# Dividing the first load of a decoder step between two DMA queues

## The chip, the cores and the metric

The kernel runs on one core of a Trainium2 chip. The metric is the device time of one execution in microseconds (us); the time of a version is the median of its runs.

## The reference: what is computed

One layer of a hybrid decoder for 256 prompt tokens and 8 sample tokens, 264 columns in all, with D = 2048, in float32:

```python
xn = rms_norm(x, g_mix);  z = xn @ w_in          # 2048 -> 3584, split among three mixers
y_pool = pool_mixer(...) @ w_pool_br             # trailing windows 2, 4, 8, 16
y_lru  = (rg_lru(causal_dwconv(u_lru)) * gelu(u_gel)) @ w_lru_br
y_conf = silu(layer_norm(causal_dwconv(c_a * sigmoid(c_b)))) @ w_conf_br
g_a, g_b, g_c = split(sigmoid(xn @ w_gate + b_gate), 3)
x = x + (g_a * y_pool + g_b * y_lru + g_c * y_conf) @ w_out
x = x + square(relu(rms_norm(x, g_mlp) @ w_up)) @ w_down      # 2048 -> 8192 -> 2048
y = rms_norm(x, g_final)
```

The outputs are y for both kinds of tokens and the new states of the mixers.

## The kernel before

Activations lie with features on the 128 partitions and the 264 tokens (N) along the row; x is 16 tiles of 128 x 264 (KD = 16). All weights are one stream of 478 chunks in the order of use, mostly of 1024 columns (CH): a pair of 128 x 512 pieces each. Every float32 product is made of three matmuls of a reduced type: the weights are split into `whi` (ScalarE, a cast, L170) and `wlo` (VectorE, the rest, L171), the activations likewise into A's upper and lower half (`x_tile`, L302 to L305). So a chunk goes HBM -> `raw` (six buffers of 1024 columns) -> ScalarE's cast -> VectorE's subtraction -> TensorE. `split(j)` does it for chunk j, three chunks ahead of its use. The order is written out by hand, per engine in program order.

The first four chunks are of kind "dual": each is one 128-row slice of w_in for two groups of 512 columns, multiplied with one tile of x as soon as it is there (`dual_mm`, L927). It takes the columns 0 to 511 first, then 512 to 1023; for each half four matmuls of whi with A's upper half, four of whi with its lower half, four of wlo with the upper half. Ahead of them stand eight warm-up products on constants (L320, two records each).

The first loads come from a DRAM array of their own, in the order of the list `HEAD`. Its entries: ("h", a, b) is columns a to b of a head row that holds g_mix (16 columns), x's first tile (264) and columns 0 to 511 of chunk 0; it goes to the last buffer of `raw`. (c, a, b) is columns a to b of chunk c; ("x", a, b) is x's tiles a to b, which go to `GX`. Eight transfers are in flight at most: a later issue waits for the one eight before it. `dma_head` issues entries, all on SyncE's queue (L156): the first ten without a wait, the others while the first chunks are split. From chunk 10 on `dma_pair(p)` brings chunks 2p and 2p + 1 (L138), in one transfer of 1 MB where both have 1024 columns, else one by one (L145). Chunks of 512 columns are 34, 37, 40, 42 (the gate blocks of the RG-LRU) and 64, which stands beside an empty one.

GpSimd copies g_mix out of the head (`gmix`, L325); VectorE prepares the first tile of x (L302), ScalarE the upper half of the others (L304).

Of the kernel before, what the change touches and what calls it, by code (L numbers as in the profile page):

```python
# [15 lines left out]
P = 128  # L16
# [3 lines left out]
N = TP + TS  # L20
KD = D // P
# [23 lines left out]
CH = 1024  # L45
# [3 lines left out]
WARM = 8  # L49
DUAL = 4  # L50
AHEAD = 3
HEAD = [("h", 0, KD + N + 256), ("h", KD + N + 256, KD + N + 512), (0, 512, CH), ("x", 1, 2)]
for _c in (1, 2):
    HEAD += [(_c, 0, 512), (_c, 512, CH), ("x", _c + 1, _c + 2)]
for _c in range(3, 9):
    HEAD += [(_c, 0, CH), ("x", 2 * _c - 2, 2 * _c)]
HEAD += [(9, 0, CH), ("x", 0, 1)]


def weight_plan():  # L60

    groups = [("w_in", 0, 16, m) for m in (1, 2, 0, 3, 4, 6, 5)]
    for g in range(4):
        groups += [("w_gate", 0, 16, t) for t in ((0, 4, 1), (5,), (2, 6), (3, 7))[g]]
        groups += [("w_pool_br", 0, 4, g), ("w_lru_br", 0, 8, g)]
    for g in range(4):
        groups += [("w_gate", 0, 16, 8 + g)]
        groups += [("w_conf_br", 0, 4, m) for m in ((), (), (0, 1), (2, 3))[g]]  # L70
    groups += [("w_out", 0, 16, m) for m in range(4)]
    for q in range(4):
        groups += [("w_up", 0, 16, q * 4 + m) for m in range(4)]
        groups += [("w_down", q * 16, 16, m) for m in range(4)]
    chunks = [("dual", 0, k, CH) for k in range(DUAL)]
    for gi, (name, _, k, m) in enumerate(groups):
        for c in range(DUAL // 2 if gi < 2 else 0, k // 2):
            chunks.append(("dense", gi, c, CH))
            if name == "w_in" and (m, c) in LRU_AT:
                chunks.append(("lru", LRU_AT.index((m, c)), 0, 512))  # L80
            if (name, m) == ("w_gate", 0) and c == 3:
                chunks += [("grp", 0, 0, 512), ("none", 0, 0, 0)]
    return groups, chunks
# [3 lines left out]
def hybrid_step(ctx: ExitStack, tc: tile.TileContext, first_in, par_in, st_in, wall, y_out, st_out):  # L87
    nc = tc.nc
# [8 lines left out]
    raw = cpool.tile([P, NRAW, CH], F32, name="raw")  # L97
# [23 lines left out]
    def acc():  # L121
        return psum.tile([P, 512], F32, name="acc", tag="acc")
# [7 lines left out]
    groups, chunks = weight_plan()  # L130
    n_pairs = len(chunks) // 2

    def dma_pair(p):
        s = (2 * p) % NRAW
        if p >= n_pairs:
            return
        if chunks[2 * p][3] == chunks[2 * p + 1][3] == CH:
            nc.sync.dma_start(raw[:, s:s + 2, :], wall[p].rearrange("p (a c) -> p a c", a=2))  # L138
        else:
            for h in range(2):  # L140
                if chunks[2 * p + h][3]:
                    dma_part(2 * p + h, 0, chunks[2 * p + h][3])

    def dma_part(c, a, b):
        nc.sync.dma_start(raw[:, c % NRAW, a:b], wall[c // 2, :, c % 2 * CH + a:c % 2 * CH + b])  # L145

    at = [0]

    def dma_head(n):
        for kind, a, b in HEAD[n]:  # L150
            if kind == "x":
                to = GX[:, KD * (a > 0) + a * N:KD + b * N]
            else:
                to = raw[:, NRAW - 1 if kind == "h" else kind % NRAW, a:b]
            w = to.shape[1]
            nc.sync.dma_start(to, first_in[at[0]:at[0] + P * w].rearrange("(p w) -> p w", p=P))  # L156
            at[0] += P * w

    head = raw[:, NRAW - 1, :]
# [149 lines left out]
        nc.vector.tensor_tensor(lo, x, f(hi), op=ALU.subtract)  # L309


    nc.scalar.preload_act_table_set(LN_EXP)
    early = HEAD.index((5, 0, CH))
    dma_head(slice(0, early))
    nc.vector.memset(ones, 1.0 / D)
    nc.vector.memset(f(ones_r), 1.0 / D)
    nc.vector.memset(eps, EPS)
# [529 lines left out]
    def half(h):  # L847
        return slice(h * (N // 2), (h + 1) * (N // 2))
# [98 lines left out]
    for a in (0, 512):  # L947
        split(2, slice(a, a + 512))
    x_tile(3)
    dma_head(slice(early, -2))  # L950
    dual = [[acc() for _ in range(4)] for _ in range(2)]
    pss = None
    for i, ch in enumerate(chunks):
# [5 lines left out]
        if i == 0:  # L959
            dma_head(slice(-2, None))  # L960
        elif i % 2 == 0:
            dma_pair((i + 8) // 2)
# [6 lines left out]
        kind, gi, c, _ = ch  # L969
# [51 lines left out]
    early = acc()  # L1021
# [4 lines left out]
    c = half(1)  # L1026
    nc.scalar.activation(total[:, c], ps[1][:, c], AF.Identity, bias=eps)
    nc.scalar.activation(X[:, KD - 1, :], X[:, KD - 1, :], AF.Copy, scale=gfin[:, KD - 1:KD])
    c = half(0)
    nc.vector.scalar_tensor_tensor(t[:, c], ps[0][:, c], EPS, sq[:, c], op0=ALU.add, op1=ALU.mult)  # L1030
    nc.vector.scalar_tensor_tensor(early[:, c], t[:, c], -3.0, rstd[:, c], op0=ALU.add, op1=ALU.mult)  # L1031
    c = half(1)
# [108 lines left out]
```

## Time and profile before

| | |
|---|---|
| time, median of 3 runs | 1300.82 us (1300.23 to 1300.83) |
| profiled execution | 1300.82 us, its span 1299.0 us |
| TensorE busy | 1288.3 us (99%) |
| VectorE, ScalarE, GpSimd busy | 837.9, 717.7, 96.9 us |
| mean clock of TensorE by the records | 0.998 |
| moved by DMA | 257.10 MB, mean 198 GB/s |

The profile counts a matmul from its start to a modelled end, so a busy TensorE may still wait for its pipeline; the spacing of its instructions tells more. "PEld" is its weight load. "SPq" and "ACTq" rows are DMA issues on SyncE's and ScalarE's queue; the landing shows in the row of the engine that waited for it. Rows of a timeline give start and length in us from the span's start, engine, line, operation, output <- input, shape, count, and in brackets how long the engine stood idle before and what ended that.

### The profile page before, as it was taken

To read this page: it belongs to the slowest core of one execution; us is meant where nothing else is said; L and a number is where in the kernel's file an instruction comes from. 1 tells how busy PE (TensorE), PEld (TensorE's weight loads), DVE (VectorE), ACT (ScalarE), POOL (GpSimd) and SP (SyncE) were. 2 spreads that over 40 slices of the span, in tenths; PEclk is the share of its full clock that TensorE was granted. 3 is DMA by queue.
4 is the path that set the end of the run, shared out by engine and by line. 5 is a ranking of instruction groups with operands and counts; after the bars stand their busy time and mean duration, and the time that the engine had idled before them with its cause. 6 is when DMAs were issued, how large, how long until landed. Compare 5 with 4: busy or idle time off the path is not lost.

```text
span 1299.0 us, 26651 instructions
## 1 busy us (share of the span) xinstructions
PE 1288.3 (99%) x11420; PEld 1287.7 (99%) x11420; DVE 837.9 (64%) x1060; ACT 717.7 (55%) x1017; POOL 96.9 (7%) x118
## 2 busy tenths in 40 slices
PE   9999999999999999999999999999999999999996
PEld 9999999999999999999999999999999999999996
DVE  7886898776777687666655455655555655555554
ACT  7767677667674655455544334543344533354544
POOL 0430010110101032021000000000000000000012
PEclk9999999999999999999999999999999999999999
DMA  9646555555655555655555555555555555555551
GB/s 360 214 169 208 188 210 200 196 194 196 228 193 198 187 182 195 217 188 201 197 196 196 195 197 196 196 190 203 196 195 196 196 197 196 196 197 196 195 197 70
DMA packets 39431, 257.10 MB, mean 198 GB/s; under 512 B 4368, under 2 KB 5648, under 8 KB 10000
## 3 DMA queue, kind: packets, MB, share of 16 engines
q1 hardware_dynamic: 38592, 253.21, 55.4%
q8 instruction: 89, 1.46, 0.4%
q10 hardware_dynamic: 576, 1.15, 0.2%
q0 software_dynamic: 144, 1.04, 0.2%
q14 instruction: 30, 0.25, 0.0%
HBM read 252.18 MB, written 3.21 MB: 197 GB/s over the span
## 4 chain that ended last, share of the span: by engine, by line
PE 99%; DVE 0%; ACT 0%; DVEq 0%; issue 0%; ACTq 0%
PE acc L195 33%; PE acc L194 33%; PE acc L193 33%; PE acc L927 1%; DVE raw L1041 0%; PE acc L320 0%; DVEq L1120 0%; PE acc L293 0%; ACT rstd L1024 0%; ACT G L1025 0%; DVE acc L1031 0%; ACT G L859 0%; DVE G L1030 0%; DVE GX L854 0%; DVE G L857 0%
## 5 line engine op out<-in xcount | busy, mean ns | idle before, releaser
L171 DVE TENSOR_TENSOR wlo<-raw,whi 128x1024 fp32r<-128x1024 f32 (+1 forms) x482 | 587.7, 1222 | 441.5 <-ACT whi L170 435.8
L170 ACT CAST whi<-raw 128x1024 fp32r<-128x1024 f32 (+1 forms) x482 | 496.4, 1032 | 530.3 <-PE acc L194 482.4
L195 PE MATMUL acc<-A,wlo 128*128 128x264 f32 x1824 | 503.4, 276 | 0.0
L194 PE MATMUL acc<-A,whi 128*128 128x264 f32 x1824 | 503.4, 276 | 0.0
L193 PE MATMUL acc<-A,whi 128*128 128x264 f32 x1824 | 503.4, 276 | 0.0
L193 PEld LDWEIGHTS acc<-A,whi 128*128 128x128 f32 x1824 | 344.7, 189 | 0.0
L194 PEld LDWEIGHTS acc<-A,whi 128*128 128x128 f32 x1824 | 344.7, 189 | 0.0
L195 PEld LDWEIGHTS acc<-A,wlo 128*128 128x128 f32 x1824 | 344.7, 189 | 0.0
L194 PE MATMUL acc<-xn,whi 128*128 128x264 f32 x1024 | 282.6, 276 | 0.0
L195 PE MATMUL acc<-xn,wlo 128*128 128x264 f32 x1024 | 282.6, 276 | 0.0
L193 PE MATMUL acc<-xn,whi 128*128 128x264 f32 x1024 | 282.6, 276 | 0.0
L193 PE MATMUL acc<-LH,whi 128*128 128x264 f32 x768 | 212.0, 276 | 0.0
L195 PE MATMUL acc<-LH,wlo 128*128 128x264 f32 x768 | 212.0, 276 | 0.0
L193 PEld LDWEIGHTS acc<-xn,whi 128*128 128x128 f32 x1024 | 193.5, 189 | 0.0
L195 PEld LDWEIGHTS acc<-xn,wlo 128*128 128x128 f32 x1024 | 193.5, 189 | 0.0
L194 PEld LDWEIGHTS acc<-xn,whi 128*128 128x128 f32 x1024 | 193.5, 189 | 0.0
L194 PE MATMUL acc<-Q,whi 128*128 128x264 f32 x644 | 177.7, 276 | 0.0
L193 PEld LDWEIGHTS acc<-LH,whi 128*128 128x128 f32 x768 | 145.2, 189 | 0.0
L195 PEld LDWEIGHTS acc<-LH,wlo 128*128 128x128 f32 x768 | 145.2, 189 | 0.0
L194 PEld LDWEIGHTS acc<-Q,whi 128*128 128x128 f32 x644 | 121.7, 189 | 0.0
L822 POOL TENSOR_TENSOR G<-G 128x264 f32<-128x264 f32 x28 | 25.5, 911 | 746.5 <-ACT G L820 745.5
L194 PE MATMUL acc<-LH,whi 128*128 128x264 f32 x256 | 70.7, 276 | 0.0
(197 smaller groups left out, 832.2 us busy)
## 6 DMA issues: line engine op xcount, KB each, us to landing
raw<-wall_dram SPq DMA_DIRECT2D x229, 1024.0 KB, 4.8
raw<-first_dram SPq DMA_DIRECT2D x7, 512.0 KB, 8.2
raw<-wall_dram SPq DMA_DIRECT2D x4, 512.0 KB, 3.7
GX<-first_dram SPq DMA_DIRECT2D x6, 264.0 KB, 7.7
raw<-first_dram SPq DMA_DIRECT2D x5, 256.0 KB, 5.0
raw<-wall_dram SPq DMA_DIRECT2D x5, 256.0 KB, 2.8
so_dram<-st POOLq DMA_DIRECT2D x1, 1018.0 KB, 6.0
st<-st_dram SPq DMA_DIRECT2D x1, 912.0 KB, 9.4
```

The costliest lines, as they stand in the source:

```text
L170: nc.scalar.copy(h[:, s], r[:, s])
L171: nc.vector.tensor_tensor(lo[:, s], r[:, s], f(h[:, s]), op=ALU.subtract)
L193: nc.tensor.matmul(ps[:, :N], whi_t, xh, start=first, stop=False)
L194: nc.tensor.matmul(ps[:, :N], whi_t, xl, start=False, stop=False)
L195: nc.tensor.matmul(ps[:, :N], wlo_t, xh, start=False, stop=last)
L822: nc.gpsimd.tensor_tensor(sq2, sq2, t, op=ALU.add)
L927: nc.tensor.matmul(ps[:, :N], w[:, k % NHI, b * P:(b + 1) * P], sent(x), start=first, stop=False)
```

## The change

The head's first entry is cut in two: g_mix and x's first tile (280 columns), issued on ScalarE's queue ahead of its activation table load, and the first 256 columns of weights, issued first on SyncE's queue. Two further entries, x's second tile and columns 0 to 511 of chunk 1, are issued on ScalarE's queue too, behind the table load. `dma_pair` brings a pair whose first chunk is full and whose second has 512 columns in one transfer.

```diff
-HEAD = [("h", 0, KD + N + 256), ("h", KD + N + 256, KD + N + 512), (0, 512, CH), ("x", 1, 2)]
+HEAD = [("h", 0, KD + N), ("h", KD + N, KD + N + 256), ("h", KD + N + 256, KD + N + 512), (0, 512, CH), ("x", 1, 2)]
...
+OTHER = (("h", 0, KD + N), ("x", 1, 2), (1, 0, 512))
...
-        if chunks[2 * p][3] == chunks[2 * p + 1][3] == CH:
-            nc.sync.dma_start(raw[:, s:s + 2, :], wall[p].rearrange("p (a c) -> p a c", a=2))
+        if chunks[2 * p][3] == CH and chunks[2 * p + 1][3]:
+            w = CH + chunks[2 * p + 1][3]
+            nc.sync.dma_start(raw.rearrange("p a c -> p (a c)")[:, s * CH:s * CH + w], wall[p, :, :w])
...
-            nc.sync.dma_start(to, first_in[at[0]:at[0] + P * w].rearrange("(p w) -> p w", p=P))
+            eng = nc.scalar if (kind, a, b) in OTHER else nc.sync
+            eng.dma_start(to, first_in[at[0]:at[0] + P * w].rearrange("(p w) -> p w", p=P))
...
+    early = HEAD.index((5, 0, CH))
+    dma_head(slice(0, 1))
     nc.scalar.preload_act_table_set(LN_EXP)
-    early = HEAD.index((5, 0, CH))
-    dma_head(slice(0, early))
+    dma_head(slice(1, early))
```

## The prediction

> **What bounds the kernel now.** I read the page's head, then busy time by stretches, then TensorE's weight loads from the start on, then the queues that feed them.
>
> ```profile
> span 1299.0 us, 26651 instructions
> PE 1288.3 (99%) x11420; PEld 1287.7 (99%) x11420; DVE 837.9 (64%) x1060; ACT 717.7 (55%) x1017; POOL 96.9 (7%) x118
> PE 99%; DVE 0%; ACT 0%; DVEq 0%; issue 0%; ACTq 0%
> ```
> ```profile
> 20.00:40.00 20.00, 20.00 (x180) 20.00 (x180) 18.39 (x25) 16.22 (x24) 0.00 (x0) 1.00 0.81 314
> 1260.00:1280.00 20.00, 20.00 (x181) 20.00 (x180) 9.94 (x11) 11.78 (x16) 4.30 (x4) 1.00 0.23 84
> ```
>
> The third line of the first fence is the chain that ended last: TensorE. The second fence holds the first and last of 63 stretches of 20 us between 20 and 1280 (columns: stretch, length, busy us and count of PE, PEld, DVE, ACT, POOL, then PE clock, DMA share, GB/s); in all 63 PE is busy throughout with 180 or 181 matmuls. So from 20 us on TensorE runs at one beat, and no earlier load can speed that up. The change can only move the moment at which the beat begins. Here are TensorE's weight loads up to there (start, length, what, count):
>
> ```profile
> 3.27 0.97 PEld L320 LDWEIGHTS acc<-const-float32-1.0 128*128 128x128 f32 x4
> 4.12 1.87 PEld L927 LDWEIGHTS acc<-A,whi 128*128 128x128 f32 x8
> 5.87 0.76 PEld L927 LDWEIGHTS acc<-A,wlo 128*128 128x128 f32 x4
> 6.81 1.05 PEld L927 LDWEIGHTS acc<-A,whi 128*128 128x128 f32 x8 [0.18 <-ACT whi L170]
> 7.79 0.53 PEld L927 LDWEIGHTS acc<-A,wlo 128*128 128x128 f32 x4
> 8.24 0.98 PEld L927 LDWEIGHTS acc<-A,whi 128*128 128x128 f32 x8
> 9.59 0.98 PEld L927 LDWEIGHTS acc<-A,whi 128*128 128x128 f32 x8
> ```
>
> Three things are to be seen. The warm-up matmuls (L320) fill TensorE until the first real load at 4.12, with no gap. Twelve loads at the beat take 9.59 - 8.24 = 1.35 us, 0.1125 each. The first twelve take from 4.12 to 5.87 + 0.76 = 6.63, or 2.51 us, nearly half speed, and then 0.18 us pass in a wait for ScalarE's cast. After 6.81 there is no wait at all. So the whole loss ahead of the beat is 2.51 - 1.35 = 1.16 us of slow matmuls and 0.18 us of waiting; only the 0.18 waits for data.
>
> What ScalarE and VectorE did:
>
> ```profile
> 0.74 1.28 ACT L312 ACT_TABLE_LOAD   x1 [0.74 <-PEq L1105]
> 3.51 0.73 ACT L170 CAST whi<-raw 128x256 fp32r<-128x256 f32 x2 [1.49 <-DMA raw<-first_dram]
> 6.36 0.40 ACT L170 CAST whi<-raw 128x256 fp32r<-128x256 f32 x1 [2.12 <-DMA raw<-first_dram]
> 6.97 0.51 ACT L304 ACTIVATE A<-GX,gmix 128x264 fp32r<-128x264 f32 x1
> 7.39 0.61 ACT L170 CAST whi<-raw 128x512 fp32r<-128x512 f32 x1
> 3.51 0.38 DVE L302 TENSOR_SCALAR A<-raw 128x264 fp32r<-128x264 f32 x1 [2.36 <-DMA raw<-first_dram]
> ```
>
> The first transfer releases both engines at 3.51; A's first tile is ready at 3.51 + 0.38 = 3.89, ahead of TensorE's 4.12. The late one is chunk 0's second half (columns 512 to 1024): its cast waits until 6.36. The casts of x's second tile (6.97) and of chunk 1's first half (7.39) follow without a gap.
>
> **The change, part by part.** The queues now:
>
> ```profile
> 0.74 1.34 SPq L156 DMA_DIRECT2D raw<-first_dram  x3
> 2.12 0.43 SPq L156 DMA_DIRECT2D GX<-first_dram  x1
> 2.60 0.91 SPq L156 DMA_DIRECT2D raw<-first_dram  x2
> 6.35 0.33 SPq L156 DMA_DIRECT2D raw<-first_dram  x1
> 1291.26 0.37 ACTq L1043 DMA_DIRECT2D y_dram<-raw  x1
> ```
> ```profile
> 1.50:2.50 1.00, 1.00 (x7) 1.00 (x6) 0.00 (x0) 0.52 (x1) 0.00 (x0) 1.00 0.64 92
> 2.50:3.50 1.00, 1.00 (x7) 1.00 (x7) 0.00 (x0) 0.00 (x0) 0.00 (x0) 1.00 1.04 373
> 3.50:4.00 0.50, 0.50 (x4) 0.50 (x4) 0.46 (x2) 0.49 (x2) 0.20 (x1) 1.00 1.13 326
> 4.00:4.50 0.50, 0.50 (x4) 0.50 (x4) 0.50 (x2) 0.24 (x1) 0.00 (x0) 1.00 1.18 144
> 4.50:5.00 0.50, 0.50 (x5) 0.50 (x4) 0.50 (x2) 0.00 (x0) 0.00 (x0) 1.00 0.74 185
> 5.00:5.50 0.50, 0.50 (x4) 0.50 (x4) 0.09 (x1) 0.00 (x0) 0.00 (x0) 1.00 0.85 286
> 5.50:6.00 0.50, 0.50 (x4) 0.50 (x4) 0.00 (x0) 0.00 (x0) 0.00 (x0) 1.00 0.97 322
> 6.00:6.50 0.50, 0.50 (x5) 0.50 (x4) 0.00 (x0) 0.14 (x1) 0.00 (x0) 1.00 1.03 377
> ```
>
> *First tile on ScalarE's queue, its weights on SyncE's.* Both halves are issued at about 0.74 instead of in one. Together they hold the bytes of the former single transfer, so they should land near 3.51. Earlier is worth nothing, since TensorE is in its warm-up until 4.12; later is free for 4.12 - 3.89 = 0.23 us. I put 0; beyond that cover each 0.1 us costs 0.1.
>
> *ScalarE's own time.* One issue goes ahead of the table load and two behind it. An issue takes 0.37 on ScalarE's queue at the end, and 1.34 / 3 = 0.45 on SyncE's at the start. Taking 0.45: table load until 0.74 + 0.45 + 1.28 = 2.47, the two issues until 3.37, the first cast at 3.51 as before. Cost 0, covered by 0.14 us of waiting and the 0.2 us above.
>
> *SyncE's queue.* Chunk 0's second half stays third, near 1.66. What follows it moves up by two issues, 0.95 us: chunk 1's second half from 3.07 to about 2.1. x's second tile (issued at 2.12 now) and chunk 1's first half (2.60) start at about 2.5 and 2.9 on ScalarE's queue, 0.3 to 0.4 later. No gain lies in issuing: the DMA share is 1.04 from 2.5 us on, so the engines, not the queue, hold the bytes back. Nor is anything further queued earlier: the eleventh issue waits until 6.35, when chunk 0's second half has landed, as it will again.
>
> *What lands when.* Sizes follow from 128 rows of 4-byte columns, in thousand bytes: head 274 and 131, chunk 0's second half 262, x's second tile 135, chunk 1's halves 262 each. The rows sum to 465 by 3.5 us, 628 by 4.0, 700 by 4.5, 793 by 5.0, 936 by 5.5, 1097 by 6.0. In order, chunk 0's second half is complete at 667, that is 4.3 us, yet its cast starts at 6.36: it lags its place by 2.1 us, through the slow stretch of 144 and 185 GB/s.
> With two queues that share evenly from 3.5 us on (ScalarE's new issues come at 2.5, and the first issue of 0.74 moved next to nothing before 1.5 to 2.5): at 3.5 us SyncE's queue has moved 465 - 143 = 322 of the 524 that it needs, 202 are left, and up to 202 of ScalarE's go between. Complete at 869 rather than 667: 5.3 us rather than 4.3, or 1.0 us later. By turns of rows, 1056 bytes of x against 2048 of weights, 101 go between: 0.6 us later. Lower end: the late shares don't recur, the wait of 0.18 goes, and the next wait is nowhere: -0.18. Upper end: +1.0, passed on to TensorE in full, since it already waits there. The 2.1 us of lag is far larger than either, so the slow stretch rather than the order sets this landing, and part of the added bytes falls inside it; I take +0.3.
> Chunk 1's first half: now complete at 1064, 5.9 us; with sharing at 540 + 719 = 1259, 6.4 us, 0.5 later. Its cast would end at 8.00 + 0.5 = 8.5 where TensorE wants it at 8.24: 0.26 late, but only as far as TensorE isn't late already. With +0.3 ahead of it: 0.
>
> The row shows full DMA engines; the Trainium skill, "DMA: Bandwidth & Descriptors" (section "Issuing engines are not separate DMA queues"), says that transfers issued by ScalarE, SyncE and GpSimd run on the same 16 engines and interleave, and that several issuers save sequencer time alone. By that rule alone the sum would be the +0.6 to +1.0 of sharing, 1301.4 to 1301.8; the trace of before has one queue at the start and can't show turns.
>
> *The pair in one transfer (dma_pair).* By the plan only one pair changes: chunks 36 (1024 columns) and 37 (512); the other mixed pairs have the 512 first. Its rows:
>
> ```profile
> 85.09 0.33 SPq L145 DMA_DIRECT2D raw<-wall_dram  x1
> 88.08 0.33 SPq L145 DMA_DIRECT2D raw<-wall_dram  x1
> 95.00 1.04 ACT L170 CAST whi<-raw 128x1024 fp32r<-128x1024 f32 x1 [0.61 <-ACT whi L170]
> raw<-wall_dram SPq DMA_DIRECT2D x229, 1024.0 KB, 4.8
> ```
>
> Chunk 36 was issued at 85.09; now it goes with chunk 37 at 88.08, when the second buffer is free. It lands at the latest 4.8 us later (time of a larger transfer), 92.9; its cast is at 95.00. Cost 0, cover 2.1 us. One SyncE issue of 0.33 is saved, off the path.
>
> **Sum.** 0 + 0 + 0.3 + 0 + 0 = +0.3 us. The profiled execution took 1300.82 us, 1.82 around its span of 1299.0; it is the median of the runs, 1300.23 to 1300.83. Forecast 1301.1, the same to what a measurement of this kernel can tell (0.2%, 2.6 us).
>
> **Rivals.**
> *R1, no effect or the wait gone.* The slow stretch doesn't recur or the halves land as before: 0 to -0.2 us, 1300.6 to 1300.8. For it: cover at every other place. Against: full DMA engines, more bytes offered beside the one late transfer.
> *R2, TensorE's slow spell ends at another moment.* The first 12 matmuls ran at 2.51 us, the next at 1.35, though the clock column of the same stretches says 1.00. If the spell ended before 4.12, 1.16 us are gained: 1299.7. If it lasted 12 more, at 1.87 / 8 = 0.23 each against 0.1125, 1.4 us are lost: 1302.2. For: a wait in this phase changes how busy TensorE is. Against: the three runs lie within 0.6 us. The Trainium skill, "TensorE: Matmul & The Clock Gate" (Part 1), says that TensorE starts at half rate until it has been busy for one free-running window of about 3.4 us; the matmul spacing agrees, and no run here shows the window move.
> *R3, slower.* Place: the cast of chunk 0's second half, 6.36. Price: each us of delay costs one. It decides when that cast begins later than 6.36 + 2.6 = 8.96, 7.3 us after the issue at 1.66 rather than 4.7: 1303.5 or more. For: such loads exist later on, when far more is queued. Against: transfers of this size take 5.0 (median of five), and sharing adds 1.0 at most.
>
> ```profile
> raw<-first_dram SPq DMA_DIRECT2D x5, 256.0 KB, 5.0
> ```
>
> **How the numbers follow.** Forecast (0 to +1.0) 0.56, R1 0.25, R2 0.13, R3 0.04, faster through something unseen 0.02: no row offers 2.6 us, as the whole loss before the beat is 1.34. Same 0.94, slower 0.04, faster 0.02. The range takes in R1, the upper end +1.0, R2's gain and most of its loss: 1299.6 to 1302.3.
>
> **What would show it.** In the profile after: 63 stretches at 180 or 181 matmuls; first real weight load at 4.1; the wait ahead of the fourth group of loads grown from 0.18 to about 0.5 with chunk 0's cast near 6.7; no new wait at chunk 36. Wrong if the cast of chunk 0's second half begins at 6.2 or before (then R1), if the first twelve loads don't take 2.5 us (R2), or if TensorE waits anywhere after 10 us.

## The result and the profile after

The changed kernel took 1302.06 us, the median of 22 runs (1300.95 to 1303.99), beside 1300.78 us for the kernel before (22 runs, 1300.21 to 1301.28). The ratio is 1.0012, 95% interval 1.0006 to 1.0017: 1.3 us slower. The forecast was 1301.1, that is 0.3 slower. The time lies inside the range given (1299.6 to 1302.3) and inside the 0.2% that the prediction called the same; but the loss is beyond the interval, and four times the term that was to make it. One run of an experiment below, "x's second tile too", took 2275.28 us at a mean granted clock of 0.556; its interval is that of the other ten.

The profiled execution took 1302.38 us with a span of 1300.6, which is 1.6 above the span of before. TensorE's weight loads at the start (start, length, what, count, and in brackets the wait and what ended it):

```profile
4.18 1.82 PEld L931 LDWEIGHTS acc<-A,whi 128*128 128x128 f32 x8
5.89 0.57 PEld L931 LDWEIGHTS acc<-A,wlo 128*128 128x128 f32 x4
8.39 1.05 PEld L931 LDWEIGHTS acc<-A,whi 128*128 128x128 f32 x8 [1.93 <-ACT whi L173]
9.36 0.53 PEld L931 LDWEIGHTS acc<-A,wlo 128*128 128x128 f32 x4
9.81 0.98 PEld L931 LDWEIGHTS acc<-A,whi 128*128 128x128 f32 x8
```

The second group for chunk 0 starts at 8.39, where it was 6.81: 1.58 us, the whole difference of the spans. Its wait is 1.93 in place of 0.18. The next group comes 1.42 us later (9.81 - 8.39; before 8.24 - 6.81 = 1.43). Every other wait of TensorE is the same, as its list of waits shows for the whole execution (what waits, for what, us in total, times, longest):

```profile
PEld acc L931 <- ACT whi L173: 1.9, 1, 1.9
PEld acc L324 <- issue: 0.8, 1, 0.8
PEld acc L1022 <- DVE G L861: 0.5, 1, 0.5
```

So one wait, once, makes the loss. ScalarE and the two queues in the same trace:

```profile
0.74 0.41 ACTq L159 DMA_DIRECT2D raw<-first_dram  x1
0.75 1.81 SPq L159 DMA_DIRECT2D raw<-first_dram  x4
1.19 1.28 ACT L317 ACT_TABLE_LOAD   x1 [1.19 <-PEq L1109]
1.22 0.42 ACTq L159 DMA_DIRECT2D GX<-first_dram  x1
1.66 0.45 ACTq L159 DMA_DIRECT2D raw<-first_dram  x1
3.48 0.40 ACT L173 CAST whi<-raw 128x256 fp32r<-128x256 f32 x1 [1.02 <-DMA raw<-first_dram]
7.93 0.71 ACT L173 CAST whi<-raw 128x256 fp32r<-128x256 f32 x2 [3.38 <-DMA raw<-first_dram]
8.55 0.51 ACT L307 ACTIVATE A<-GX,gmix 128x264 fp32r<-128x264 f32 x1
8.96 1.12 ACT L173 CAST whi<-raw 128x512 fp32r<-128x512 f32 x2
```

ScalarE's issues of x's second tile (1.22) and chunk 1's first half (1.66) lie inside the table load (1.19 to 2.47), not behind it. The cast of chunk 0's second half waits for its transfer until 7.93, before 6.36. What comes after it (x's second tile at 8.55, chunk 1 at 8.96) had landed by then: no further wait.

It isn't that fewer bytes came in. Stretches from the start on, first two of before, then two of after (the last column is GB/s):

```profile
0.00:6.00 6.00, 5.22 (x24) 5.25 (x25) 1.85 (x7) 2.02 (x3) 0.74 (x8) 1.00 0.69 183
0.00:8.00 8.00, 7.22 (x37) 7.06 (x38) 3.06 (x10) 3.66 (x7) 0.74 (x8) 1.00 0.77 226
```
```profile
0.00:6.00 6.00, 5.22 (x24) 5.25 (x25) 1.85 (x7) 2.09 (x3) 0.74 (x8) 1.00 0.68 197
0.00:8.00 8.00, 5.87 (x28) 5.71 (x28) 1.85 (x7) 2.16 (x4) 0.74 (x8) 1.00 0.77 238
```

By 6 us the changed kernel had moved 197 x 6 = 1182 thousand bytes, before 1098; by 8 us 1904 against 1808. More arrived, and the one transfer that TensorE was waiting for arrived later. The trace's semaphore steps (each transfer is reported in 16 shares, one per DMA engine) give it in more detail: of this transfer 14 shares had landed at 4.49 before and the last at 6.33; after, 14 at 6.31 and the last two at 6.95 and 7.91.

### The profile page after: what moved, and what is told of

Its sections match the earlier page's. It is cut to its first block, busy times and chain, and to the rows that moved or that the text cites. A ratio compares the mean times of both kernels' runs of the same rounds, so it can differ in the third digit from the quotient of the medians.

```text
span 1300.6 us, 26651 instructions
## 1 busy us (share of the span) xinstructions
PE 1288.1 (99%) x11420; PEld 1287.6 (99%) x11420; DVE 837.2 (64%) x1060; ACT 717.4 (55%) x1017; POOL 96.9 (7%) x118
## 4 chain that ended last, share of the span: by engine, by line
PE 98%; DMA 0%; DVE 0%; ACT 0%; SPq 0%; DVEq 0%; issue 0%; ACTq 0%
PE acc L198 33%; PE acc L197 33%; PE acc L196 33%; PE acc L931 1%; DMA raw<-first_dram 0%; DVE raw L1045 0%; SPq L159 0%; DVEq L1124 0%; PE acc L296 0%; ACT whi L173 0%; ACT rstd L1028 0%; ACT G L1029 0%; DVE acc L1035 0%; ACT G L863 0%; DVE G L1034 0%
```

## The experiments

Sixteen measurements of eleven runs each were made, of fourteen new kernels and, once more, of two kernels measured earlier, beside the kernel before on the same chip (its medians there: 1300.67, 1300.68, 1300.57, 1300.65 for the four groups below). Edits are shown against the changed kernel unless said otherwise; OTHER is the list of what goes on ScalarE's queue. "The late cast" is the first cast of chunk 0's second half, in one profiled run of each; it varies from run to run (6.36 before, 5.64 with the pair alone, whose start is the same), so the medians decide.

### First group: which part does it

**Head alone.** Only x's first tile stays on ScalarE's queue.

```diff
-OTHER = (("h", 0, KD + N), ("x", 1, 2), (1, 0, 512))
+OTHER = (("h", 0, KD + N),)
```

> Only the first tile of x stays on ScalarE's queue; x's second tile and chunk 1's first half go back to SyncE's. Theory A (their bytes, issued at 1.22 and 1.66 us, share the DMA engines with chunk 0's second half, issued at 1.66): its cast, at 7.93 us in the changed kernel, starts between 6.0 and 6.7 again, TensorE waits at most 0.5 us for it, and the time is 1300.5 to 1301.1. Theory B (a second queue, or the head cut into two transfers, slows the start by itself): cast at 7.3 or later, time 1301.7 or more.

Measured 1300.57 us, ratio 0.9999 [0.9990, 1.0008]. The late cast begins at 5.53. Dividing the head costs nothing.

**x's second tile too.** OTHER = (("h", 0, KD + N), ("x", 1, 2)).

> x's first and second tile on ScalarE's queue, chunk 1's first half back on SyncE's, behind chunk 0's second half. Theory A, by bytes: 135 of the former 397 thousand bytes are still ahead of or beside chunk 0's second half; its cast starts about a third of the way from 6.4 to 7.9, at 6.7 to 7.1; time 1300.9 to 1301.5. Theory B: as the changed kernel, cast at 7.3 or later, time 1301.7 or more.

Measured 1300.37 us, 0.9997 [0.9988, 1.0006]; late cast 5.79, no wait in TensorE: less than either theory gave. So the first two issues don't make the loss; the third, chunk 1's first half, does.

**Chunk 0's second half ahead of both**, all four on ScalarE's queue:

```diff
-OTHER = (("h", 0, KD + N), ("x", 1, 2), (1, 0, 512))
+OTHER = (("h", 0, KD + N), (0, 512, CH), ("x", 1, 2), (1, 0, 512))
```

> As the changed kernel, but chunk 0's second half goes on ScalarE's queue too, right behind x's first tile and ahead of x's second tile and chunk 1's first half, so it is issued at 1.22 us and has half the engines. Theory A: it no longer stands behind the 262 thousand bytes of the first weights; its cast starts at 6.2 or earlier, TensorE's wait for it is 0.2 us or less, and the time is 1300.4 to 1300.9, with x's second tile and chunk 1's first half still in time. Theory B: cast at 7.3 or later, time 1301.7 or more.

Measured 1302.63 us, 1.0017 [1.0008, 1.0026]: a miss. Chunk 0 did come early; chunk 1 came late instead. ScalarE and its queue, then TensorE, in this trace:

```profile
3.53 0.33 ACTq L159 DMA_DIRECT2D raw<-first_dram  x1
3.90 1.35 ACT L173 CAST whi<-raw 128x256 fp32r<-128x256 f32 x4 [1.44 <-DMA raw<-first_dram]
9.21 1.14 ACT L173 CAST whi<-raw 128x512 fp32r<-128x512 f32 x2 [2.26 <-DMA raw<-first_dram]
```
```profile
9.87 0.97 PEld L931 LDWEIGHTS acc<-A,whi 128*128 128x128 f32 x8 [2.64 <-ACT whi L173]
10.77 0.73 PEld L931 LDWEIGHTS acc<-A,wlo 128*128 128x128 f32 x4
```

All four casts of chunk 0 run in one go from 3.90, the late one at 4.54. But by the time of ScalarE's fourth issue eight transfers are out (three on its queue, five on SyncE's), so chunk 1's first half goes only at 3.53 instead of 1.66, when the first have landed, and TensorE waits 2.64 us for it. The eleven runs also fall in two groups, seven at 1302.03 to 1302.73 and four at 1304.00 to 1304.31; the profiled one (1304.12) is of the upper, and its stretches show why:

```profile
8.00:10.00 2.00, 0.12 (x1) 0.13 (x2) 0.14 (x1) 0.80 (x2) 0.00 (x0) 1.00 0.98 373
10.00:12.00 2.00, 2.00 (x14) 2.00 (x15) 2.00 (x4) 2.00 (x5) 0.00 (x0) 0.76 0.92 310
12.00:14.00 2.00, 2.00 (x11) 2.00 (x10) 1.99 (x4) 1.97 (x4) 0.00 (x0) 0.50 1.02 405
14.00:16.00 2.00, 2.00 (x18) 2.00 (x17) 2.00 (x4) 1.89 (x4) 0.00 (x0) 0.89 1.04 415
```

After the wait the granted clock (third column from the end) falls to 0.50, and 11 matmuls go in 2 us instead of the 18 of the beat (2 / 0.1125). The trace's clock records put the half rate at 3.41 us, from 11.04 on; half of that, 1.7 us, is about the distance of the two groups (1.8 between their means).

**The pair alone**: the kernel before with the new `dma_pair` and nothing else.

> The kernel before with the changed dma_pair alone, so that chunks 36 and 37 come in one transfer. Theories A and B alike: chunk 36 still lands about 2 us ahead of its cast, nothing waits, 1300.8, within 0.4 us of the kernel before. Rival C (the later transfer of chunk 36 is what costs): 1301.5 or more.

Measured 1300.77 us, 1.0000 [0.9991, 1.0009]. It costs nothing, as forecast.

### Second group: is it chunk 1's first half, its bytes, or what it shares with

**Chunk 1's first half without x's second tile.** OTHER = (("h", 0, KD + N), (1, 0, 512)); its issue is then second in ScalarE's queue, at 1.21.

> x's first tile and chunk 1's first half on ScalarE's queue (issued at 1.2 us), x's second tile back on SyncE's. Theory A, now narrower (what holds chunk 0's second half is chunk 1's first half, 262 thousand bytes in the other queue at the same time): its cast starts at 7.0 to 8.0 us, TensorE waits 1.0 us or more for it, time 1301.4 to 1302.4. Theory D (three issues on ScalarE's queue, whatever their bytes, slow the start): two issues, so cast at 6.5 or earlier, 1300.2 to 1300.8.

Measured 1300.32 us, 0.9998 [0.9989, 1.0007]; late cast 5.87 (the profiled run, at 1300.91, is its slowest). The same 262 thousand bytes on the same queue cost nothing when they are issued at 1.21. The theory that these bytes on ScalarE's queue are enough for the loss is refuted. (The packet records, below, show that they moved mostly ahead of chunk 0's second half, not beside it.)

**Half of it.** x's second tile and columns 0 to 255 of chunk 1 on ScalarE's queue:

```diff
+_i = HEAD.index((1, 0, 512))
+HEAD[_i:_i + 1] = [(1, 0, 256), (1, 256, 512)]
-OTHER = (("h", 0, KD + N), ("x", 1, 2), (1, 0, 512))
+OTHER = (("h", 0, KD + N), ("x", 1, 2), (1, 0, 256))
```

> As the changed kernel, but chunk 1's first half is cut in two: columns 0 to 255 on ScalarE's queue, 256 to 511 on SyncE's in their old place, one transfer more. Theory A: half of the bytes, half of the delay; cast of chunk 0's second half between 6.3 and 7.2 us, time 1300.7 to 1301.4. Theory D: three issues on ScalarE's queue as in the changed kernel, cast at 7.3 or later, time 1301.7 or more.

Measured 1301.19 us, 1.0005 [0.9996, 1.0014]; late cast 6.47, TensorE waits 0.93. In between, though the interval includes 1.

**Chunk 0's second half alone on ScalarE's queue**, behind x's first tile: OTHER = (("h", 0, KD + N), (0, 512, CH)).

> x's first tile and chunk 0's second half on ScalarE's queue, everything else on SyncE's in the old order: the one late transfer gets a queue to itself. Theory A: it lands near 4.5 us, as with all four there, and chunk 1's first half, issued near 2.1 on SyncE's queue, lands by 7.4, in time; TensorE waits for neither more than 0.3 us; time 1300.0 to 1300.6, as good as or better than both kernels. Theory D says the same; theory B (a second queue is slow by itself): 1301.7 or more.

Measured 1300.03 us, 0.9996 [0.9987, 1.0005]. Its ScalarE and TensorE rows:

```profile
4.36 1.02 ACT L173 CAST whi<-raw 128x256 fp32r<-128x256 f32 x3 [0.65 <-DMA raw<-first_dram]
```
```profile
4.12 2.07 PEld L931 LDWEIGHTS acc<-A,whi 128*128 128x128 f32 x8
6.08 0.85 PEld L931 LDWEIGHTS acc<-A,wlo 128*128 128x128 f32 x4
6.85 0.98 PEld L931 LDWEIGHTS acc<-A,whi 128*128 128x128 f32 x8
8.20 0.97 PEld L931 LDWEIGHTS acc<-A,whi 128*128 128x128 f32 x8
```

Three casts follow each other from 4.36 on; the late one is the second, at 4.67, 1.7 us earlier than before, and TensorE waits for nothing. What is left is TensorE's own slow first twelve.

**The wait filled**: as with all four on ScalarE's queue, and eight products on constants, in columns that nothing reads, stand on TensorE between chunk 0 and chunk 1.

```diff
+            if c == 0:
+                for _ in range(8):
+                    nc.tensor.matmul(dual[1][3][:, 384:512], one, one, start=False, stop=False)
```

> The version with chunk 0's second half ahead on ScalarE's queue (1302.03 to 1302.73 in seven runs, 1304.0 to 1304.31 in four; TensorE waited 2.64 us for chunk 1 in its profile, and the clock column then fell to 0.50) with eight constant products more, about 1.7 us at full speed, placed on TensorE where it waits. They write to columns that nothing reads. Theory E (the upper group is the clock that falls back after the wait): no run near 1304, all at 1302.0 to 1303.0. Rival F (the upper group is a later landing of the data): the upper group stays, about a third of the runs above 1303.5.

Measured 1302.47 us (1302.12 to 1302.73), 1.0014 [1.0005, 1.0023]. All eleven runs lie in the lower group. The constants in the trace, the first loads after them, and the stretch that was at half rate:

```profile
7.46 1.86 PEld L978 LDWEIGHTS acc<-const-float32-1.0 128*128 128x128 f32 x16
9.67 0.97 PEld L931 LDWEIGHTS acc<-A,whi 128*128 128x128 f32 x8 [0.35 <-ACT whi L173]
```
```profile
12.00:14.00 2.00, 2.00 (x20) 2.00 (x19) 1.98 (x3) 2.00 (x5) 0.00 (x0) 1.00 1.01 363
```

The data come no sooner (9.67), but the clock stays at 1.00 from 12 to 14 us. So the upper group of that version is the clock falling back after a long wait. That the four runs of the changed kernel at 1303.70 to 1303.99 have the same cause is argued: they lie about 1.9 us above the others, show a lower mean clock (0.996 against 0.997 or 0.998), and the kernel has a long wait at the same stage; none of them was profiled.

### Third group: place, number, moment

**The change again.**

> The changed kernel once more, for a second profile of it. All theories that put the loss into the late last share of chunk 0's second half: its cast at 7.0 us or later, TensorE's wait 1.0 us or more, 1301.5 to 1302.5. Rival N (the first profile was a poor draw and the loss lies elsewhere): a cast before 6.7 with a time above 1301.5.

Measured 1301.93 us, 1.0013 [1.0004, 1.0022]. In this trace (1301.51, the fastest of its runs) the late cast begins at 7.04 and the first twelve loads ran faster:

```profile
4.12 1.19 PEld L931 LDWEIGHTS acc<-A,whi 128*128 128x128 f32 x8
5.23 0.53 PEld L931 LDWEIGHTS acc<-A,wlo 128*128 128x128 f32 x4
7.49 1.05 PEld L931 LDWEIGHTS acc<-A,whi 128*128 128x128 f32 x8 [1.73 <-ACT whi L173]
```

**The two exchanged**: chunk 1's first half second in ScalarE's queue (1.22), x's second tile third (1.67).

```diff
+_i = HEAD.index((1, 0, 512))
+HEAD[_i - 1:_i + 1] = [(1, 0, 512), ("x", 1, 2)]
```

> As the changed kernel with the last two issues on ScalarE's queue swapped: chunk 1's first half at 1.22 us, x's second tile at 1.66. Theory G (what ScalarE's queue issues at the same moment as chunk 0's second half, 1.66, holds it: now 135 thousand bytes instead of 262): its cast between 6.0 and 6.8, time 1300.4 to 1301.2. Theory D (three issues, or all 540 thousand bytes on that queue): cast at 7.0 or later, 1301.5 or more.

Measured 1301.33 us, 1.0005 [0.9996, 1.0014]; late cast 6.66. Like the half: 135 thousand bytes third in the queue cost about what 131 do, 0.5 to 0.8 us, neither beyond its interval.

**Chunk 0's second half in place of chunk 1's first**: OTHER = (("h", 0, KD + N), (0, 512, CH), ("x", 1, 2)).

> Three issues on ScalarE's queue: x's first tile, chunk 0's second half, x's second tile; chunk 1's first half on SyncE's at 1.66 us. Theory G (bytes and order): chunk 0's second half lands before 4.8 as in the version without x's second tile, chunk 1's first half by 7.2, no wait over 0.3 us, 1300.0 to 1300.6. Theory D (three issues there are what is slow): one of the two late, a wait of 0.7 us or more, 1301.2 or more.

Measured 1300.76 us, 1.0002 [0.9993, 1.0011]; the profiled run, at 1301.73, is its slowest. There chunk 0's second half is in time (its cast at 4.65), x's second tile, third in the queue, comes only at 8.08, and TensorE waits 1.05 us at chunk 1:

```profile
8.08 0.52 ACT L307 ACTIVATE A<-GX,gmix 128x264 fp32r<-128x264 f32 x1 [2.73 <-DMA GX<-first_dram]
```

**A small load in between**: x's second tile stays on SyncE's queue, an unused load of 64 bytes a row takes its place.

```diff
+    nc.scalar.dma_start(rstd[:, 0:16], par_in[:, 0:16])
-OTHER = (("h", 0, KD + N), ("x", 1, 2), (1, 0, 512))
+OTHER = (("h", 0, KD + N), (1, 0, 512))
```

> x's first tile, then a load of 64 bytes per row that nothing needs, then chunk 1's first half on ScalarE's queue, the last at 1.66 us together with chunk 0's second half; x's second tile on SyncE's. Theory G (the moment decides): cast of chunk 0's second half at 7.0 or later, 1301.3 or more, though the queue holds no more bytes than the version with chunk 1's first half at 1.21 us, which took 1300.32. Theory T (it takes all 540 thousand bytes): cast at 6.5 or earlier, 1300.9 or less.

Measured 1302.03 us, 1.0010 [1.0001, 1.0019]. Two rows of the two versions side by side, first the one without the small load, then with it:

```profile
1.21 0.42 ACTq L159 DMA_DIRECT2D raw<-first_dram  x1
5.87 0.71 ACT L173 CAST whi<-raw 128x256 fp32r<-128x256 f32 x2 [1.06 <-DMA raw<-first_dram]
```
```profile
1.66 0.45 ACTq L159 DMA_DIRECT2D raw<-first_dram  x1
7.01 0.71 ACT L173 CAST whi<-raw 128x256 fp32r<-128x256 f32 x2 [2.66 <-DMA raw<-first_dram]
```

Eight thousand bytes more, but chunk 1's first half issued 0.45 later and third: the whole loss is back, without x's second tile. It is not the total of bytes on ScalarE's queue.

### Fourth group: the moment without a third issue, and the times that the prediction assumed

Here ScalarE is held back by a fill on VectorE and a copy of one element that waits for it.

**Chunk 1's first half held to 1.58**, second in the queue:

```diff
+    nc.vector.memset(Gf[:, 2640:2640 + 640], 0.0)
+    nc.scalar.copy(G[:, 18, 0:1], Gf[:, 2640:2641])
-OTHER = (("h", 0, KD + N), ("x", 1, 2), (1, 0, 512))
+OTHER = (("h", 0, KD + N), (1, 0, 512))
```

> Two issues on ScalarE's queue, x's first tile and chunk 1's first half (1300.32 when issued at 1.21), the second held back to about 1.6 to 1.8 us with a shorter scratch fill. Theory G: cast of chunk 0's second half at 6.8 or later, 1301.3 or more. Theory D (it takes three issues): cast at 6.4 or earlier, 1300.8 or less.

Measured 1300.92 us, 1.0002 [0.9993, 1.0011]; late cast 6.51, wait 1.31 (longer than the loss, because the loads ahead of it ended early here). Its median is 0.6 above the version at 1.21 and 1.1 below the one with the small load: between the theories.

**x's second tile at 1.22, chunk 1's first half held to 2.79**, third in the queue.

```diff
-    dma_head(slice(1, early))
+    third = HEAD.index((1, 0, 512))
+    dma_head(slice(1, third))
+    nc.vector.memset(Gf[:, 2640:2640 + 1800], 0.0)
+    nc.scalar.copy(G[:, 18, 0:1], Gf[:, 2640:2641])
+    dma_head(slice(third, early))
```

> Three issues on ScalarE's queue; x's second tile at 1.22 as in the changed kernel, chunk 1's first half held back to about 2.5 us. Theory G: cast of chunk 0's second half at 5.5 to 6.6; chunk 1's first half lands between 7 and 8; 1300.4 to 1301.3. Theory D: cast at 7.0 or later, 1301.6 or more.

Measured 1300.89 us, 1.0003 [0.9994, 1.0012]; the profiled run, 1301.67, is its slowest, with the late cast at 6.91 and a wait of 1.42. Third in the queue, yet mostly without the loss.

**Both near the times that the prediction had assumed** (issued at 2.79 and 3.16, against about 2.5 and 2.9):

```diff
+    nc.vector.memset(Gf[:, 2640:2640 + 1800], 0.0)
+    nc.scalar.copy(G[:, 18, 0:1], Gf[:, 2640:2641])
```

> The changed kernel with its last two issues on ScalarE's queue held back to about 2.5 and 2.9 us, where the prediction had put them: VectorE first fills a scratch area (1800 columns), ScalarE copies one column of it, and the issues stand behind that. Theory G (what is issued at the same moment as chunk 0's second half, 1.66, holds it): its cast back at 5.5 to 6.6 us; time 1300.5 to 1301.3, near the forecast of 1301.1, unless chunk 1's first half is late in its place. Theory D (three issues on ScalarE's queue): as the changed kernel, cast at 7.0 or later, 1301.6 or more.

Measured 1301.74 us, 1.0013 [1.0003, 1.0022]. Queue, ScalarE and TensorE in its trace:

```profile
2.79 0.34 ACTq L159 DMA_DIRECT2D GX<-first_dram  x1
3.16 0.45 ACTq L159 DMA_DIRECT2D raw<-first_dram  x1
5.59 0.71 ACT L173 CAST whi<-raw 128x256 fp32r<-128x256 f32 x2 [1.22 <-DMA raw<-first_dram]
7.75 0.51 ACT L307 ACTIVATE A<-GX,gmix 128x264 fp32r<-128x264 f32 x1 [1.45 <-DMA GX<-first_dram]
9.06 0.97 PEld L933 LDWEIGHTS acc<-A,whi 128*128 128x128 f32 x8 [1.51 <-ACT whi L173]
```

Chunk 0's second half comes earlier than before (5.59 against 6.36; TensorE, early itself, waits 0.43 us), but now x's second tile and chunk 1 are late, and TensorE waits 1.51 us there. The loss moved from one chunk to the next.

**Chunk 0's second half alone, again.**

> The version with x's first tile and chunk 0's second half on ScalarE's queue once more (1300.03 against 1300.68 before), for a second profile and more runs. Theories G and D alike: cast of chunk 0's second half before 5.0, no wait over 0.3 us, 1299.9 to 1300.4, below the kernel before.

Measured 1300.44 us, 0.9996 [0.9987, 1.0005]. In both measurements together, 22 runs between 1299.67 and 1300.92, it has the lowest median of all versions; the interval includes 1 both times, so that it beats the kernel before is not shown. In this trace the late cast is at 4.59 and TensorE starts its second group at 5.76, 1.05 earlier than before, but the span is only 0.3 shorter (1298.7): two waits for VectorE's `wlo`, 0.37 us at 18.61 and 0.22 us at 37.92, take part of it back.

## Why the prediction was wrong, by its own steps

- *What bounds the kernel, and that only the start of the beat can move*: right for this change. In the trace after, all 63 stretches of 20 us hold 180 or 181 matmuls, and one wait ahead of 8.39 accounts for the span. For an earlier start it is not the whole story. With the head alone the second group of loads starts at 5.99, 0.82 earlier than before, yet the span is only 0.1 shorter (1298.9): further on, at 38.16, TensorE waits 0.48 us for VectorE's `wlo`, which it does not do before. A row of its timeline, and one of its list of waits:

```profile
5.99 1.05 PEld L931 LDWEIGHTS acc<-A,whi 128*128 128x128 f32 x8 [0.49 <-ACT whi L173]
PEld acc L198 <- DVE wlo L174: 0.5, 1, 0.5
```

- *First tile divided, 0*: right. First cast 3.48, first real weight load 4.18; the head alone 1300.57.
- *The pair in one transfer, 0*: right; 1300.77, and no new wait at chunk 36.
- *When ScalarE issues*: wrong. The two issues were put behind the table load, at 2.5 and 2.9. They went at 1.22 and 1.66, about 0.9 us before their old moments (2.12, 2.60) instead of 0.3 to 0.4 after. So the sum was made for another order: chunk 1's first half went out at the same moment as chunk 0's second half. For the order that ran, the prediction's own even sharing gives far more than +0.3. SyncE's 524 thousand bytes up to this transfer then share with all 540 of ScalarE's queue and are complete at 1048 rather than 667: by the rows of before at about 5.9 us rather than 4.3, 1.6 later (an estimate).
- *The wait for chunk 0's second half, +0.3*: this is the term that failed. The direction, the place (the cast of 6.36) and that the delay passes to TensorE in full came right, the place in part by luck: near the times that the prediction had assumed, this transfer was not late (5.59) and the loss arose at chunk 1. The size was wrong: the medians differ by 1.28 us, and the late cast moved by 0.68 (6.36 to 7.04) and by 1.57 (to 7.93) in the two profiles. The working had +0.6 to +1.0 from sharing, and talked itself down to +0.3 with the argument that the slow stretch rather than the order sets this landing. (It also read the DMA engines as full from 2.5 us on, where its own rows have shares of 0.74 and 0.85 from 4.5 to 5.5.) The trace after refutes that argument: the stretch was filled (295 in place of 185 GB/s from 4.5 to 5.0 us) and the landing went back. Even the upper end was too low. The trace after has moved the 1048 thousand bytes at about 5.5 us (190 GB/s to there), 1.2 us after the 4.3 of before, and the last share came 2.4 us later, at 7.91; before, it lagged by 2.1. So in this trace most of the delay is the order, and the lag hardly grew.

```profile
0.00:5.50 5.50, 4.72 (x22) 4.75 (x23) 1.85 (x7) 2.09 (x3) 0.74 (x8) 1.00 0.68 190
```

- *Chunk 1's first half, 0.26 late at the assumed times, put at 0*: wrong too, though the change never got there. Issued 0.3 us later than that, it left TensorE waiting 1.51 us at chunk 1 (1301.74).
- The Trainium skill, "DMA: Bandwidth & Descriptors" ("Issuing engines are not separate DMA queues"): its rule of interleaving, which the prediction set beside its own +0.3 at +0.6 to +1.0, was nearer, and the trace after agrees: from 3.75 to 5.5 us 96 packets of 2 KB ended on ScalarE's queue, 133 on SyncE's. What the section says of the gain, that several issuers save the issue time alone, doesn't cover the experiment in which one transfer's queue changed which data came first (late cast 4.67 against 6.36).
- *R1, no effect*: refuted by the interval. *R3, slower by over 0.2%*: the late cast stayed below 8.96 in both profiles.
- *R2, the slow spell*: in part. The eight loads from 4.1 on took between 0.98 and 2.07 us from profile to profile, so the spell does end at different moments. The trace's clock records show when: the first one at full rate begins at 6.34 before and 5.96 after, and anywhere from 3.73 to 6.91 in the eighteen profiles (4.01 where the eight loads took 0.98, 6.72 where they took 2.07). The clock column prints 1.00 also ahead of the first record, so it could not show the spell. But an early end gained next to nothing: with the head alone TensorE, after a wait of 0.49 for data, was 0.82 us ahead at 5.99 and only 0.1 at the end, with the wait for VectorE in between. No run shows the 1.16 us of R2. R2's loss may have come in another form, half rate once more after a long wait, in 4 of 22 runs; the median of the other 18 is 1301.88, so those four put about 0.2 of the 1.28 on the median.

*The cause, as far as it goes.* Shown: the loss is one wait for data in the first 10 us; in the change the full loss takes chunk 1's first half on ScalarE's queue behind another issue (without it 1300.37, without that issue 1300.32; ahead of that issue 1301.33, part of the loss and within its interval). It isn't the second queue as such, nor the bytes alone: the same transfer at 1.21, at 1.58 and behind a small load at 1.66 gave 1300.32, 1300.92 and 1302.03. The loss hits what lands last, chunk 0's second half, or x's second tile and chunk 1. Every version that lost beyond its interval had at least three issues on ScalarE's queue by 3.6 us and none with one or two did, but of the seven with three, two (1300.89 and 1300.76) lost hardly anything.

Whether the moment or the number of issues does it, no run separates cleanly, but the packet records speak for the moment. Chunk 1's packets ran from 2.85 to 4.27 us where they cost nothing, mostly ahead of chunk 0's second half (its first packet at 3.84); in the change they ran from 3.81 to 7.65, beside it. Thousand bytes that ended on ScalarE's queue from 4.0 to 5.5 us, in the versions that leave chunk 0's second half on SyncE's queue, beside the time of the same profiled run:

| version | bytes | time |
|---|---|---|
| head alone; x's second tile too | 0; 0 | 1300.70; 1300.37 |
| chunk 1 at 1.21; held to 1.58 | 38; 51 | 1300.91; 1300.95 |
| half of chunk 1; the two exchanged | 102; 151 | 1301.18; 1301.13 |
| the change, twice; small load | 194, 167; 188 | 1302.38, 1301.51; 1301.78 |
| chunk 1 held to 2.79 | 30 | 1301.67 |

In all but the last, bytes and time rise together (but for 0.05 us between two); there chunk 1's packets came after 4.63, beside the end of the transfer, whose last share came at 6.88. The stretch was chosen after the fact, and the version near the assumed times (0 bytes) lost its time at another chunk, so this is an argument and no test. Open too is why the last of the 16 shares trail. A packet of 2 KB mostly takes 0.084 us, but single ones took up to 1.33 us before (4.36 to 5.69) and 1.74 us after (4.70 to 6.44); what held them no run shows.

## What to carry to other kernels

Where a first load is divided, try giving the second queue the transfer that the bottleneck waits for next (here chunk 0's second half: 1300.03 and 1300.44, no loss, a gain not shown), and leave what is needed later behind it in the old queue. Here a transfer that was needed later, on the other queue, competed with the urgent one (1302.06); behind it in the same queue it did not (1300.37). Judge by the landing of the last share of that one transfer, not by bytes per second: more bytes came here, and the kernel waited longer. When the working of a term gives 0.6 to 1.0, don't take 0.3 for a reason that no row has tested.

## What had not been expected of the hardware

- DMA issues on ScalarE's queue go out while the table load runs: 1.22 and 1.66, the load from 1.19 to 2.47.
- A wait of TensorE of 2.64 us was followed in the profiled run by 3.41 us at half the granted clock, which cost 1.7 us; in 7 of 11 runs, by their times, it was not. The Trainium skill, "TensorE: Matmul & The Clock Gate" (Part 1), has the fallback after an idle window of about 3.4 us; here the gap in the weight loads was shorter, and with eight constant products in it all eleven runs stayed in the lower group.
- Eight loads of the same kind at the start took 0.98 and 2.07 us in two runs whose times differ by 0.1 us (1300.70 and 1300.81).
- An earlier start is kept only in part: the 0.82 us that the head alone gained at 5.99 were 0.1 at the end of the same trace, where 0.44 with x's second tile too (chunk 1's loads at 7.80 against 8.24) were still 0.4.
